# Unread matmuls at the start, gate columns before value products, pooling tiles at the head of the fill, and the first half's last rows two products sooner, in a two-layer decoder trunk

## The chip, the cores and the metric

One Trainium2 chip, one of its cores. The metric is the device time of one execution in microseconds (us). The engines are PE (TensorE: matrix products and transposes), ACT (ScalarE), DVE (VectorE), POOL (GpSimd) and SP (SyncE, which here only issues DMAs).

## The reference, cut to what matters

One inference step of a decoder of two layers, for a prompt of 512 rows and a sample group of 8 x 4 rows that share all weights (544 columns in all; the model's width is 1024, its inner width 2816). All is float32.

```python
h = rmsnorm(x, g_mix)
z = h @ w_in                       # cut by columns among mixers and gates
u_pool, q_raw, kv_raw, nsa_gate, c_b, c_c, c_x, gate_pool, gate_nsa, gate_conv = split_columns(z)
y_pool = pool_mixer(u_pool, ...)   # trailing means over 2/4/8/16 rows, minus the row, a map per group, a scale
y_nsa  = nsa_mixer(q_raw, kv_raw, nsa_gate, ...)  # compressed blocks, selected blocks, window; a gate per head
y_conv = c_b * conv3(c_c * c_x)
merged = sum(sigmoid(gate_b) * (y_b @ w_br_b) for the three branches)
x = x + merged @ w_out
x = x + (silu(conv3(hf @ W_a)) * (hf @ W_b)) @ W_down     # hf = rmsnorm(x, g_ffn)
# after the layers: a final rmsnorm of both groups' rows; caches and states are outputs too
```

## The kernel before, in words

Activations lie with channels on the 128 partitions and the 544 rows of prompt and sample along the free axis, in two halves of 272. A product takes one tile of 128 output channels: for each half and each of the 8 tiles of the 1024 input channels there are three matmuls (L323, L324, L326), since each operand is split into a high and a low part: high x high, high x low, low x high. So a full product is 48 matmuls of 128 x 128 weights and 272 columns.

The program is a list of tasks, which `tasks` makes for each layer. A task is a product, its weights, and a function that takes the result out of PSUM (`evac`). Weights come by a DMA on SP into one of 3 raw buffers, three tasks ahead (`look`); ACT casts the high part (L298), and DVE, or POOL while the attention heads run, subtracts to get the low part (L299). The gate columns of the sparse attention (`zng`, 24 of them) have weights of their own: `stacked_weights` sets a tile to zero on POOL (L316), copies the high part on ACT (L317) and subtracts the low part on DVE (L318), so that each k takes two matmuls. Products accumulate in one of 3 PSUM buffers `g`. There are two buffers each for transposes (`PT`) and for attention scores (`PS`), and 8 work tiles `W`.

The order on PE is written out by hand and is the order in which the program emits. On the other engines a planner sets the order from its own costs; only in `setup` ACT and SP go in written order too. `later(n, ...)` puts work n ticks ahead, and a tick is one half product.

Each layer has three stages. Stage "z": the normalised input's products: zkc, zvc, zks (their start also makes the norm), zkw, four zq, then zvs and zvw (the values of the selected and the window keys), zng (the gate columns), a conv tile c, two cmp products (block compression, from `cmp_split`: L532 casts on ACT and L534 subtractions on DVE, 8 of each, on pages that DMAs L455 bring), a conv tile x, and two cmp products. What stands behind zng: `nsa_gates` evacuates on ACT and DVE (L688, L689, L690), ends with a tanh (L692) and a DVE step (L693); `nsa_rows` transposes on PE (L700) two ticks later.

Stage "fill": conv b of tile j = 0, then c, x, b of j = 1, then pairs of a gate and a branch product (first the eight of the conv branch, then the pooling branch). These are pumped between the steps of the attention: first the sample's (L729 to L803; `L767`, `L769`, `L771` scale, the transposes L776 read), then 8 heads, with a fixed amount of product time per step. The two pooling tiles zpool stand in it behind six gates. `pool_mix` evacuates them (L643 to L645 on DVE), adds shifted copies of the columns on POOL (L654 and L655), and makes mean minus token on DVE (L662 to L667); `pool_map` follows 9 and 10 ticks later.

Stage "rest": the branch products of the attention, `w_out`, and the FFN in chunks of ups and downs. In the last chunk of the last layer the eight down products are made by halves: first half 0 of all eight, then half 1. `final_tile` adds the residual (L1238) and sums squares (L1246). `final_sum` gives 1/rms by Newton steps on DVE (L377 to L383); `final_rows` spreads them over the rows with a PE product (L393), multiplies on POOL (L1262) or DVE (L1264) and stores (L1266). `fl` holds how many half 1 products stand between half 0's last product and its `final_sum` and `final_rows`.

Of the kernel before, what the change touches and what calls it, by code (L numbers as in the profile page):

```python
# [6 lines left out]
F32 = mybir.dt.float32  # L7
F32R = mybir.dt.float32r
# [8 lines left out]
NP = 512  # L17
# [199 lines left out]
class Task:  # L217
    def __init__(self, name, evac, w, x, m, pre, mode, stage, halves, keep):
        self.name, self.evac, self.w, self.x, self.m = name, evac, w, x, m
        self.pre, self.mode, self.stage, self.halves, self.keep = pre, mode, stage, halves, keep  # L220
# [1 line left out]


class Trunk:
    def __init__(self, tc, ins, outs, ctx, slots=49, work=8, fill=1.66, look=3, lag=3, np_=4, nps=2, pm=9, ng=3, raw=3, by_pool=((0, 1, 2, 3, 4, 5, 6, 7), (1, 3, 5)), fl=(2, 7, 6, 1), ys=(4.0, 3.0, 10.0, 3.0, 3.0, 3.5)):
        self.tc, self.nc, self.i, self.o = tc, tc.nc, ins, outs
        pool = lambda name, **k: ctx.enter_context(tc.tile_pool(name=name, **k))
        self.cp = pool("cp", bufs=1)
        self.wp = pool("wp", bufs=4)
        self.bp = pool("bp", bufs=3)  # L230
        self.tp = pool("tp", bufs=slots)
        self.kp = pool("kp", bufs=work)
        self.dp = pool("dp", bufs=1, space=bass.MemoryType.DRAM)
        self.sp = pool("sp", bufs=2)
        self.ps = pool("ps", bufs=1, space=bass.MemoryType.PSUM)
        self.n = 0
        self.ng, self.raw = ng, raw
        self.by_pool, self.fl, self.ys_ = by_pool, fl, ys
        self.np_, self.nps, self.pm = np_, nps, pm
        self.fill, self.look, self.lag = fill, look, lag  # L240


    def nm(self, p):
# [155 lines left out]
    def setup(self):  # L399
        nc, i = self.nc, self.i  # L400
        self.cst = self.cp.tile([128, CS_W], F32, name="cst")
        self.norms = self.cp.tile([128, NM_W], F32, name="norms")
        self.ones = self.cp.tile([128, 2], F32, name="ones")
        self.vc = self.cp.tile([128, 256], F32R, name="vc").rearrange("p (g n) -> p g n", g=2)
        self.cT = self.cp.tile([128, 512], F32R, name="cT")
        self.ptt = self.cp.tile([1, 16], I32, name="ptt")
        self.cst1 = self.cst2 = None
        nc.vector.memset(self.ones, 1.0)
        nc.scalar.activation(self.ones[:, 1:2], self.ones[:, 0:1], AF.Tanh)
        self.x = [self.T() for _ in range(KT)]  # L410
        self.ident = self.c("ident")
        nc.gpsimd.memset(self.vc[64:128].bitcast(F32), 0.0)
        nc.gpsimd.memset(self.cT[64:128].bitcast(F32), 0.0)
        s, v, g = nc.scalar, nc.vector, nc.gpsimd
        by = ((s, None), (s, v), (g, None), (s, v), (s, v), (g, g), (s, v), (s, v))
        ap = self.tl[0].w[0]
        r = self.raw_weights(8)
        for t, a in ((self.norms, i["norms"]), (self.x[0], i["xT"][:, 0]), (r[:, 0:4], ap[:, 0:4]),
                     (self.x[1], i["xT"][:, 1]), (r[:, 4:8], ap[:, 4:8])):
            nc.sync.dma_start(t, a)  # L420
        for k in range(2, 7):
            nc.sync.dma_start(self.x[k], i["xT"][:, k])
        self.norm_tile(0, 0, "g_in")
        w = self.weight_parts(r, 0, 4)
        self.norm_tile(1, 0, "g_in")
        self.got[0] = w + self.weight_parts(r, 4, 8)
        self.nxt = 1
        for k in range(2, 7):
            self.norm_tile(k, 0, "g_in")
        for k in range(3):  # L430
            self.square_sum(self.x[k], k, *by[k])
        self.ahead(2)
        nc.sync.dma_start(self.x[7], i["xT"][:, 7])
        nc.sync.dma_start(self.cst, i["cst"])
        nc.sync.dma_start(self.ptt, i["pt"])
        for u in range(3, 7):
            self.square_sum(self.x[u], u, *by[u])
        self.norm_tile(7, 0, "g_in")
        self.square_sum(self.x[7], 7, *by[7])
# [522 lines left out]
    def tasks(self, l):  # L962
        nc, i = self.nc, self.i
# [3 lines left out]
        def add(name, evac, w, x=h, m=128, pre=None, mode=None, stage="rest", halves=(0, 1), keep=None):  # L967
            T.append(Task(f"{name}.{l}", evac, w, x, m, pre, mode, stage, halves, keep))

        def zt(m):  # L970
            return (i["w_in"][l, m], 8)

        def store(name, j, t):
            nc.sync.dma_start(self.o[name][l, j], t)
# [63 lines left out]
        def raw_v(name, out, j, e0):  # L1038
            def evac(ps):
                z = self.z_raw(ps)  # L1040
                store(out, j, z)
                nc.gpsimd.tensor_copy(self.Ev[:, :, e0:e0 + 4], self.seq4(z))
                self.later(2, lambda: setattr(self, name, self.v_stack(z)))
            return evac

        add("zvs", raw_v("vsel", "kvT", 3, 16), zt(8), stage="z")
        add("zvw", raw_v("vwin", "wT", 1, 20), zt(9), stage="z")

        def gates(ps):
            z = self.nsa_gates(ps)  # L1050
            self.later(2, lambda: self.nsa_rows(z))
            self.later(3, self.nsa_sample)

        add("zng", gates, (i["w_ng"][l], 8), m=64, stage="z")
        self.hid = [None] * 2

        def cmp(st, a):
            def evac(p):
                if a == 1:
                    self.hid[st] = self.gelu(p)  # L1060
            return evac

        def conv(j, nme):
            def evac(ps):
                self.zz[nme] = self.z_raw(ps)
                if nme == "b":
                    self.yc[j] = self.conv_mix(j, self.zz["c"], self.zz["x"], self.zz["b"])
                    if j == 1:
                        nc.sync.dma_start(self.o["co"][l], self.coO)
            return evac  # L1070

        for j in range(2):
            for u, nme in enumerate("cxb"):
                add("zconv", conv(j, nme), zt(10 + 3 * j + u), stage="z" if j == 0 and u < 2 else "fill")
                if j == 0 and u < 2:
                    for a in range(2):
                        add("cmp", cmp(u, a), (i["cw1"][l, u][:, 8 * a:8 * a + 8], 8),
                            x=lambda a=a: self.cmpx[8 * a:8 * a + 8],
                            pre=(lambda st=u: self.cmp_split(st)) if a == 0 else None, mode=f"cmp{a}", stage="z")


        def gate(key, m):
            def evac(ps):
                t = self.T() if self.mg[m] is None or key == "n" and m > 1 else self.W()
                self.halves(ps, lambda p, cs: nc.vector.tensor_mul(t[:, cs], p, self.r[:, cs]))
                nc.scalar.activation(t, t, AF.Tanh, scale=0.5)
                self.gt[key, m] = t
            return evac
# [12 lines left out]
                    nc.gpsimd.tensor_add(self.mg[m], self.mg[m], t)  # L1101
            return evac

        def pool(j):
            def evac(ps):
                pd = self.pool_mix(j, ps)
                for hf in range(2):
                    self.later(self.pm + hf, lambda hf=hf: self.pool_map(j, pd, hf))
            return evac

        kinds = {"c": (18, 0, lambda: self.yc), "p": (26, 2, lambda: self.yp), "n": (34,)}
        seq = [(key, m) for key in "cp" for m in range(8)]
        for n, (key, m) in enumerate(seq + [("n", 0)]):
            if n == 6:
                for j in range(2):
                    add("zpool", pool(j), zt(16 + j), stage="fill")
            add("gate", gate(key, m), zt(kinds[key][0] + m), stage="fill")
            if n > 0:
                key, m = seq[n - 1]
                k0, x = kinds[key][1:]  # L1120
                add("branch", branch(key, m), (i["br_a"][l, m, :, k0:k0 + 2], 2), x=x, stage="fill")
# [303 lines left out]
```

## Time and profile before

| | |
|---|---|
| median of 3 runs (lowest, highest) | 1763.63 us (1761.86, 1764.05) |
| the profiled execution's own time | 1759.85 us |
| its span in the profile | 1758.0 us |
| PE, PE weight load, DVE, ACT, POOL busy | 97%, 96%, 65%, 42%, 28% |
| chain that ended last, by engine | PE 87%, DVE 7%, SP's queue 2%, DMA 2% |
| DMA | 175.52 MB, 100 GB/s on average |

How to read it: the span runs from the profile's start to its last event, and the execution's time is a little more. Busy shares are of the span; loading of weights into PE overlaps its matmuls. Engines wait for each other through semaphores; the profile infers what ended a wait.

### The profile page before, as it was taken

The page shows a single profiled execution, that of the slowest core. Times are in us where ns is not written, and L with a number is a line of the kernel's source. Part 1 is how long each engine was busy: PE and PEld are TensorE (multiplying, and loading weights), DVE is VectorE, ACT ScalarE, POOL GpSimd, SP SyncE. Part 2 cuts the span into 40 slices and gives each one's busy share as a digit, 9 for nine tenths or more (in the row PEclk, how much of TensorE's full clock was granted, in tenths as well). Part 3 has the DMA queues.
Part 4 walks back from the last instruction along what each step waited for, and adds up shares of the span by engine and source line. Part 5 has one row for each costly group of instructions (what it writes and reads, how often), then busy time and mean ns, then how long its engine had stood idle before and what let it go on. Part 6 is the DMA issues. An engine that isn't in the chain of part 4 may idle for free.

```text
span 1758.0 us, 35101 instructions
## 1 busy us (share of the span) xinstructions
PE 1710.2 (97%) x13488; PEld 1689.6 (96%) x13488; DVE 1145.0 (65%) x2552; ACT 737.2 (42%) x1499; POOL 487.4 (28%) x719
## 2 busy tenths in 40 slices
PE   8999989999999999999998998999999999999996
PEld 8999989999999999999998998999999999999996
DVE  6675888856566565565857568887564665565566
ACT  5443555643333233233435345666333333232333
POOL 3212655630122121121231226456001321121113
PEclk9999999999999999999999999999999999999998
DMA  6653211224222322322465532112242222323322
GB/s 216 178 183 113 68 47 46 64 78 150 89 85 74 107 77 86 100 77 77 152 176 148 186 116 49 46 49 64 78 153 90 86 83 91 91 79 97 91 75 78
DMA packets 97208, 175.52 MB, mean 100 GB/s; under 512 B 31250, under 2 KB 51858, under 8 KB 97042
## 3 DMA queue, kind: packets, MB, share of 16 engines
q1 hardware_dynamic: 97042, 173.29, 32.5%
q8 instruction: 107, 1.75, 0.4%
q14 instruction: 59, 0.48, 0.1%
HBM read 157.19 MB, written 12.71 MB: 97 GB/s over the span
## 4 chain that ended last, share of the span: by engine, by line
PE 87%; DVE 7%; SPq 2%; DMA 2%; ACT 1%; issue 1%; POOL 0%; DVEq 0%; ACTq 0%; POOLq 0%
PE pg L323 25%; PE pg L324 25%; PE pg L326 25%; PE ps L830 2%; PE po L910 2%; PE pt L872 2%; SPq L483 1%; SPq L455 1%; DVE mx L846 1%; PE ps L323 1%; PE ps L324 1%; PE ps L326 1%; PE ps L1328 1%; PE ps L1329 1%; PE ps L1330 1%
## 5 line engine op out<-in xcount | busy, mean ns | idle before, releaser
L323 PE MATMUL pg<-t,wh 128*128 128x272 f32 x3824 | 1122.1, 294 | 19.8 <-DVE t L1093 8.3
L324 PE MATMUL pg<-t,wh 128*128 128x272 f32 x3824 | 1104.5, 289 | 0.7 <-DVE t L1225 0.7
L326 PE MATMUL pg<-t,wl 128*128 128x272 f32 x3792 | 1097.3, 289 | 0.0
L323 PEld LDWEIGHTS pg<-t,wh 128*128 128x128 f32 x3824 | 722.7, 189 | 24.6 <-DVE t L1093 8.8
L324 PEld LDWEIGHTS pg<-t,wh 128*128 128x128 f32 x3824 | 723.2, 189 | 2.4 <-DVE t L1225 1.0
L326 PEld LDWEIGHTS pg<-t,wl 128*128 128x128 f32 x3792 | 718.1, 189 | 0.2 <-DVE wl L299 0.2
L298 ACT CAST wh<-wr 128x512 fp32r<-128x512 f32 (+2 forms) x528 | 316.8, 602 | 581.8 <-PE pg L324 464.1
L299 DVE TENSOR_TENSOR wl<-wr,wh 128x512 fp32r<-128x512 f32 (+2 forms) x432 | 299.9, 696 | 164.8 <-ACT wh L298 146.3
L1139 DVE TENSOR_TENSOR t<-t,pg 128x272 f32<-128x272 f32 x204 | 89.1, 437 | 99.4 <-PE pg L326 97.6
L1176 POOL TENSOR_TENSOR W<-W,W 128x512 f32<-128x512 f32 x44 | 78.1, 1776 | 229.6 <-ACT wh L298 200.7
L299 POOL TENSOR_TENSOR wl<-wr,wh 128x512 fp32r<-128x512 f32 (+1 forms) x96 | 114.7, 1197 | 70.1 <-ACT wh L298 64.0
L616 POOL COPY t<-W 128x2 f32<-128x2 f32 x44 | 9.9, 225 | 369.6 <-DVE W L1159 333.0
L859 POOL TENSOR_SCALAR P<-P,ls,gate 128x128 f32<-128x128 f32 (+3 forms) x128 | 79.9, 625 | 95.7 <-DVE ls L857 61.4
L852 ACT ACTIVATE P<-ps,mx 128x256 f32<-128x256 f32 (+1 forms) x144 | 71.4, 498 | 45.7 <-DVE mx L846 33.2
L342 DVE TENSOR_TENSOR t<-W,t 128x544 fp32r<-128x544 f32 x48 | 34.9, 727 | 81.2 <-ACT t L341 81.1
L363 POOL TENSOR_TENSOR t<-t,W 128x544 f32<-128x544 f32 x19 | 26.6, 1399 | 207.4 <-ACT W L354 207.4
L874 ACT CAST b<-pt 128x128 fp32r<-128x128 f32 (+3 forms) x128 | 54.0, 422 | 49.7 <-PE pt L872 49.0
L875 DVE TENSOR_TENSOR b<-pt,b 128x128 fp32r<-128x128 f32 (+3 forms) x128 | 62.0, 485 | 16.6 <-ACT b L874 14.9
L830 PE MATMUL ps<-t,Q 128*128 128x288 f32 (+6 forms) x288 | 64.0, 312 | 4.7 <-ACT P L852 3.6
L341 ACT CAST t<-W 128x544 fp32r<-128x544 f32 x48 | 31.1, 647 | 87.0 <-POOL W L1177 82.5
L846 DVE TENSOR_REDUCE mx<-ps 128x1 f32<-128x256 f32 (+1 forms) x144 | 64.5, 448 | 2.3
L1166 ACT ACTIVATE W<-W 128x560 f32<-128x560 f32 x44 | 29.6, 673 | 74.8 <-DVE W L606 74.8
(254 smaller groups left out, 1833.5 us busy)
## 6 DMA issues: line engine op xcount, KB each, us to landing
wr<-up SPq DMA_DIRECT2D x88, 512.0 KB, 3.6
wr<-w_in SPq DMA_DIRECT2D x83, 512.0 KB, 3.8
wr<-down SPq DMA_DIRECT2D x64, 256.0 KB, 2.7
wr<-w_out SPq DMA_DIRECT2D x16, 512.0 KB, 3.6
wr<-down SPq DMA_DIRECT2D x32, 192.0 KB, 2.4
t<-xT SPq DMA_DIRECT2D x16, 272.0 KB, 5.7
b<-pgA SPq DMA_DIRECT2D x64, 64.0 KB, 2.7
wr<-cw SPq DMA_DIRECT2D x8, 512.0 KB, 3.7
```

The costliest lines, as they stand in the source:

```text
L298: nc.scalar.copy(h, r[:, k0:k1])
L299: (eng or nc.vector).tensor_sub(w, r[:, k0:k1], h)
L323: self.nc.tensor.matmul(p[:m, :HF], wh, xh[:, cs], start=a, stop=False)
L324: self.nc.tensor.matmul(p[:m, :HF], wh, xl[:, cs], start=False, stop=b and wl is None)
L326: self.nc.tensor.matmul(p[:m, :HF], wl, xh[:, cs], start=False, stop=b)
L830: nc.tensor.matmul(p[:, :n], q[:, 128 * i:128 * i + 128], kd[:, c0:c0 + n], start=u == 0, stop=u == 1)
L846: nc.vector.tensor_reduce(mx[:, u:u + 1], p[:, c0:c0 + m], axis=AX.X, op=OP.max, negate=True)
L852: nc.scalar.activation(t[:, pos:pos + m], p[:, c0:c0 + m], AF.Exp, bias=mx[:, 0:1], accum_out=ls[:, u:u + 1])
L859: nc.gpsimd.tensor_scalar(t[:, 0:n], t[:, 0:n], ls[:, 0:1], self.gate[:, i, 1 + kk, hd:hd + 1], op0=OP.mult, op1=OP.mult)
L875: nc.vector.tensor_sub(blk(pt)[:, lo][:, ::-1], blk(p)[:, 0:i + 1], blk(pt)[:, hi])
L1139: self.halves(ps, lambda p, cs: nc.vector.tensor_add(self.x[m][:, cs], self.x[m][:, cs], p))
L1176: nc.gpsimd.tensor_mul(f[:, 0:NP], t[:, 0:NP], z[:, 0:NP])
```

## The change

It has four parts. (A) `setup` sets a work tile to 1.0 on DVE and issues 11 matmuls of 128 x 128 weights and 512 columns on it, whose result nobody reads. (B) The task zng stands before zvs and zvw and not behind them. (C) The two zpool tasks stand directly behind conv b of j = 0, the first task of the fill, and not behind the sixth gate; `pool` is only moved up, so that it is defined in time. (D) `fl[1]` is 5 and not 7: `final_rows(0)` is emitted two half 1 products sooner.

```diff
-    ... fl=(2, 7, 6, 1), ys=(4.0, 3.0, 10.0, 3.0, 3.0, 3.5)):
+    ... fl=(2, 5, 6, 1), warm=11, ys=(4.0, 3.0, 10.0, 3.0, 3.0, 3.5)):
...
         self.ident = self.c("ident")
+        warm = self.W(NP, F32R)
+        nc.vector.memset(warm.bitcast(F32), 1.0)
+        p = self.PT()
+        for _ in range(self.warm):
+            nc.tensor.matmul(p, warm[:, 0:128], warm, start=True, stop=True)
...
-        add("zvs", raw_v("vsel", "kvT", 3, 16), zt(8), stage="z")
-        add("zvw", raw_v("vwin", "wT", 1, 20), zt(9), stage="z")
...
         add("zng", gates, (i["w_ng"][l], 8), m=64, stage="z")
+        add("zvs", raw_v("vsel", "kvT", 3, 16), zt(8), stage="z")
+        add("zvw", raw_v("vwin", "wT", 1, 20), zt(9), stage="z")
...
         for j in range(2):
+            if j == 1:
+                for n in range(2):
+                    add("zpool", pool(n), zt(16 + n), stage="fill")
             for u, nme in enumerate("cxb"):
                 add("zconv", conv(j, nme), zt(10 + 3 * j + u), stage="z" if j == 0 and u < 2 else "fill")
...
         for n, (key, m) in enumerate(seq + [("n", 0)]):
-            if n == 6:
-                for j in range(2):
-                    add("zpool", pool(j), zt(16 + j), stage="fill")
             add("gate", gate(key, m), zt(kinds[key][0] + m), stage="fill")
```

## Rows read from the trace of the kernel before

**Rows 1.** The page's line of busy time, share of the span, and instructions.

```profile
PE 1710.2 (97%) x13488; PEld 1689.6 (96%) x13488; DVE 1145.0 (65%) x2552; ACT 737.2 (42%) x1499; POOL 487.4 (28%) x719
```

**Rows 2.** PE's waits: who released it; us in total, times, longest.

```profile
PE pg L323 <- DVE t L1093: 8.3, 2, 4.2
...
PE pt L700 <- DVE W L693: 5.8, 2, 3.3
PE po L393 <- DVE ny L383: 4.1, 1, 4.1
PE pg L323 <- DVE wh L318: 3.8, 2, 2.0
```

**Rows 3.** Stretches: length, busy PE PEld DVE ACT POOL, PEclk, DMA share, GB/s.

```profile
5.98:15.78 9.80, 9.10 (x37) 8.55 (x38) 9.11 (x10) 9.11 (x15) 5.13 (x4) 1.00 0.91 355
...
89.58:94.88 5.30, 5.30 (x26) 5.12 (x24) 5.30 (x11) 5.30 (x9) 0.00 (x0) 0.68 0.30 99
955.60:959.41 3.81, 3.81 (x27) 3.61 (x25) 3.81 (x9) 3.81 (x7) 0.00 (x0) 1.00 0.30 85
232.05:237.64 5.59, 5.59 (x24) 5.56 (x25) 4.25 (x16) 2.63 (x7) 2.29 (x3) 0.50 0.01 4
...
203.00:232.00 29.00, 24.43 (x190) 23.59 (x188) 26.48 (x75) 15.33 (x41) 22.53 (x30) 0.98 0.22 50
...
118.00:142.00 24.00, 24.00 (x201) 22.90 (x200) 14.88 (x38) 11.05 (x28) 8.57 (x19) 1.00 0.45 139
142.00:170.00 28.00, 28.00 (x278) 26.79 (x278) 13.68 (x42) 9.66 (x25) 5.43 (x8) 1.00 0.45 147
1097.24:1101.20 3.96, 3.79 (x17) 3.49 (x18) 3.90 (x14) 1.59 (x4) 1.71 (x2) 0.57 0.01 2
```

**Rows 4.** Instructions at the start: start us, us, engine, line, count, idle before.

```profile
8.82 6.11 DVE L1225 SCALAR_TENSOR_TENSOR t<-t,norms,t 128x544 fp32r<-128x544 f32 x5
```

**Rows 5.** Instructions around the gate columns, and the page's line of their neighbours' DMA.

```profile
71.09 2.95 ACT L532 CAST b<-b 128x326 fp32r<-128x326 f32 x4 [7.36 <-DMA b<-pgA]
73.94 0.35 ACT L317 CAST wh<-wr 128x192 fp32r<-128x192 f32 x1
...
66.80 0.35 SPq L313 DMA_DIRECT2D wr<-w_ng  x1
...
82.99 4.83 DVE L534 TENSOR_TENSOR t<-b,b 128x326 fp32r<-128x326 f32 x7
...
935.50 5.92 ACT L532 CAST b<-b 128x326 fp32r<-128x326 f32 x8 [4.77 <-DMA b<-pgA]
...
wr<-w_in SPq DMA_DIRECT2D x83, 512.0 KB, 3.8
```

**Rows 6.** Lines from 203 to 232 (busy, mean ns), then sample attention's instructions.

```profile
L654 POOL TENSOR_TENSOR W<-W 128x526 f32<-128x526 f32 (+3 forms) x6 | 6.6, 1107 | 0.9 <-DVE pf L645 0.9
...
L662 DVE SCALAR_TENSOR_TENSOR W<-W,W 64x512 f32<-64x512 f32 x4 | 3.7, 936 | 0.1
...
L645 DVE TENSOR_TENSOR pf<-pg,t 128x32 f32<-128x32 f32 x2 | 0.4, 180 | 0.0
...
133.92 2.23 POOL L771 TENSOR_SCALAR W<-W,sfc 128x256 f32<-128x256 f32 x2
137.63 0.60 PE L776 MATMUL pt<-cst,W 128*128 128x128 f32 x4
```

**Rows 7.** Instructions of the last rows, on DVE, PE and POOL.

```profile
1737.42 0.16 DVE L382 TENSOR_TENSOR nt<-nt,nv 128x3 f32<-128x3 f32 x1
...
1737.89 0.15 DVE L383 SCALAR_TENSOR_TENSOR ny<-nt,ny 128x3 f32<-128x3 f32 x1
...
1739.58 0.49 PE L393 MATMUL po<-cst,ny 128*128 128x128 f32 x3
...
1740.75 6.17 POOL L1262 TENSOR_TENSOR W<-t,W 128x272 f32<-128x272 f32 x8 [5.49 <-ACT W L396]
...
1746.26 0.68 DVE L382 TENSOR_TENSOR nt<-nt,nv 128x3 f32<-128x3 f32 x1
```

More of the change, by code (lines that the diff above doesn't have):

```diff
@@ L224, with __init__ @@
 class Trunk:
-    def __init__(self, tc, ins, outs, ctx, slots=49, work=8, fill=1.66, look=3, lag=3, np_=4, nps=2, pm=9, ng=3, raw=3, by_pool=((0, 1, 2, 3, 4, 5, 6, 7), (1, 3, 5)), fl=(2, 7, 6, 1), ys=(4.0, 3.0, 10.0, 3.0, 3.0, 3.5)):
+    def __init__(self, tc, ins, outs, ctx, slots=49, work=8, fill=1.66, look=3, lag=3, np_=4, nps=2, pm=9, ng=3, raw=3, by_pool=((0, 1, 2, 3, 4, 5, 6, 7), (1, 3, 5)), fl=(2, 5, 6, 1), warm=11, ys=(4.0, 3.0, 10.0, 3.0, 3.0, 3.5)):
         self.tc, self.nc, self.i, self.o = tc, tc.nc, ins, outs
@@ L239, in __init__ @@
         self.np_, self.nps, self.pm = np_, nps, pm
-        self.fill, self.look, self.lag = fill, look, lag
+        self.fill, self.look, self.lag, self.warm = fill, look, lag, warm
     def nm(self, p):
@@ L1070, in conv, with pool, evac @@
             return evac
+        def pool(j):
+            def evac(ps):
+                pd = self.pool_mix(j, ps)
+                for hf in range(2):
+                    self.later(self.pm + hf, lambda hf=hf: self.pool_map(j, pd, hf))
+            return evac
         for j in range(2):
+            if j == 1:
+                for n in range(2):
+                    add("zpool", pool(n), zt(16 + n), stage="fill")
             for u, nme in enumerate("cxb"):
@@ L1102, in branch @@
             return evac
[L1104 to L1109, printed above, removed]
         kinds = {"c": (18, 0, lambda: self.yc), "p": (26, 2, lambda: self.yp), "n": (34,)}
```

## The prediction

> **What bounds the kernel now.** I read the busy line first: PE is busy 97% of the span, no other engine over 65%, and a matmul takes 1710.2 / 13488 = 0.127 us [rows 1]. The reader is to see that no product gets shorter here: only PE's idle time, and the time it runs at half clock, can be won. Next the list of what PE waited for [rows 2]: few waits, each with a cause; those of two come in pairs of like size, one per layer. Then a table of stretches [rows 3], for the price of the low clock and for how full the other engines are beside each wait. Last the instructions at each place [rows 4 to 7].
>
> The profiled execution took 1759.85 us (span 1758.0), the median shown is 1763.63, 3.78 more. I form the sum against the profiled one and take it off the median unchanged.
>
> **A. Eleven unread matmuls at the start.** They add a DVE memset and 11 PE instructions ahead of the first product at 5.98, where PE has nothing else. In the first stretch PE issued 37 matmuls in 9.80 us, 9.10 of it busy: 0.246 us each, twice the 0.127 [rows 1, 3], so the start runs at 1.2 GHz, though this row prints 1.00. A matmul of 512 columns in place of 272 is then 0.46 us, eleven 5.1. If the memset is over by 1.2 they end near 6.3, some 0.3 late, or earlier if the clock rises under them. What full clock wins is small, since the x tiles come from DVE: five of them leave it between 8.82 and 14.93 whatever PE does [rows 4]. Only the work after 14.93 gets shorter: until 15.78 these are 3 to 4 matmuls at 0.12 too much each, 0.4 us, and the 0.70 us that the first stretch idles stay. I take +0.3. Ends: +0.7 (the idle time too), and -1.5: PE waits more between those tiles at full clock, and if the clock falls there it costs what the layer 0 stretch below lost.
>
> **B. Gate columns ahead of value products.** The gate product (zng) gets its weights through a POOL memset, the ACT copy L317 and the DVE subtraction L318. In ACT's order L317 stands behind four page casts L532, 2.95 us from 71.09, and runs at 73.94 [rows 5]; PE waits for L318 3.8 us in the two layers [rows 2]. After the product, L693 must give the gate rows to the transposes L700, but seven subtractions L534, 4.83 us from 82.99, are ahead of it on DVE [rows 5]: 5.8 us in two [rows 2]. After layer 0's wait the clock is at half: 26 matmuls took 5.30 us, layer 1's 27 took 3.81 [rows 3], so 1.5. Together 3.8 + 5.8 + 1.5 = 11.1 us.
>
> Two products earlier, zng's weights are wanted before any page cast is due (their DMA, issued at 66.80, goes some 12 us up), and the transposes, two ticks after the product, stand behind all of zvs: L693 has 48 matmuls, 6.1 us, and comes ahead of the L534 block. Both old waits should go. Late next is zvw. L317 ends at 74.3 and PE had then waited nearly 2, so zvw ended near 73; zng now starts two products before, at 61, and with its 32 matmuls and zvs's 48 PE wants zvw at 71. Its DMA takes zng's slot in SP's queue behind the page loads: 66.80 plus 3.8 to landing [rows 5] is 70.6, and a cast and a subtraction (0.74 us each, as one page cast) make it 72: 1 us late per layer. If its cast, or the gates' copies and tanh on ACT, stand behind four page casts, it is 2.95 more, behind all eight 5.92 [rows 5]. I charge 2 per layer, the sure 1 and a third of 2.95: B = 11.1 - 4 = 7. Ends: +11.1, and -4, where both layers pay 5.92 and half of the clock term again (11.1 - 11.8 - 3).
>
> **C. Pooling tiles at the head of the fill.** The two zpool products and their evacuations now stand among the heads, directly before the wait for L1093, 8.3 us in two [rows 2]. From 203 to 232 DVE is busy 26.48 of 29.00 us, POOL 22.53, while PE has 24.43 [rows 3]. Seven pooling lines (L643 to L667; the first and the last by time are shown) are 9.9 us of DVE's [rows 6]. Without them DVE has 16.6 us of work where PE has 24.4: both waits lose their cause. With them goes the half clock behind them: 5.59 us at 0.50 lost 2.8, 3.96 at 0.57 lost 1.7 [rows 3]. Gross 8.3 + 4.5 = 12.8 us.
>
> The new place is behind the first conv b product, in 118 to 170. There DVE has 14.88 of 24.00 and 13.68 of 28.00 us, POOL 8.57 and 5.43 [rows 3]. With 9.9 more, DVE has 38.5 of 52; with six L654 (6.6 [rows 6]), POOL has 20.6: PE's own work covers both. Not covered is what must come on time: sample attention's POOL step L771 ends at 133.92 + 2.23 = 136.15, and the transpose L776 that reads it is at 137.63 [rows 6]. That is 1.5 us of slack; one L654 is 1.1, two in front of it are past it. SP gets two small stores per tile there, and the two tiles' weight loads ahead of the conv and gate weights they change places with: as many in all, so I cost them at nothing; a weight 1 us late would show as a wait for a cast. I charge one miss of 1 us per layer, and 0.5 for the gates that take the pooling tiles' place: 12.8 - 3 = 9.8. Ends: +12.8, and -3, where the wait with its clock only moves and two such misses come on top in one layer and one in the other.
>
> One rule speaks against C. DVE ops beside POOL's adds run long: in the tail L382 took 0.68 us while POOL worked and 0.16 before POOL began [rows 7]. The Trainium skill, "SBUF — State Buffer", section "Who interferes with whom", has it that a DVE instruction with two SBUF inputs and a GpSimd instruction that reads SBUF lock each other out for a whole instruction. The trace agrees by these 0.52 us; by this rule the sum is rival 2's, by the engines' busy shares it is the one below.
>
> **D. First half's last rows two products sooner.** final_rows(0) comes after 5 and not 7 of the second half's eight products. Its eight POOL multiplications L1262 run from 1740.75 for 6.17 us [rows 7], to 1746.92, beside the Newton steps for which PE waits last, 4.1 us [rows 2]. Of these L382 took 0.68 us at 1746.26, but 0.16 when the first half's ran at 1737.42 [rows 7]; I count three steps so stretched, 3 x 0.52 = 1.5. Two products are 2 x 9 x 0.127 = 2.3 us: POOL ends near 1744.6, before these steps, if nothing else runs there. In return PE meets the first half's L393, now at 1739.58, at 1737.3, and the Newton step that it reads ends at 1737.89 + 0.15 [rows 7]: 0.7 late, in PE's own order, so paid in full, unless the steps come earlier too. 1.5 - 0.7 = 0.8, of which I take 0.5, since the moved multiplications meet L1238 and L1246 instead. Ends: +1.5 and -0.8.
>
> **Sum.** 0.3 + 7.0 + 9.8 + 0.5 = 17.6 us: 1742.3 on the profiled execution, 1763.63 - 17.6 = 1746.0 on the median.
>
> **Rivals.**
> - R1, four casts: zvw's cast or the gates' tanh lands behind four page casts in both layers, 2.95 + 1 per layer. B = 11.1 - 8 = 3, time 1750. For it: in layer 1 ACT ran the eight casts in one piece, 5.92 us [rows 5]. Against: in layer 0 the first starts at 71.09, when zng's product has long ended.
> - R2, POOL against DVE: each moved POOL add holds DVE as L382 was held, for its whole length. In 118 to 170 DVE is then taken for 38.5 + 6.6 = 45.1 of 52 us, 87%, near the 91% of the stretch where the wait arose, and a wait of 3.4 us comes per layer. C = 3, time 1753. Against: PE's buffers carry it over single waits, and no head needs DVE at once there.
> - R3, the other side: the planner puts all eight page casts ahead of the gate product's ACT copies. Its two halves hold two of the three g buffers, so zvs's second half stops for 5.9 us, and L693's old wait and zvw's late weights come behind (3.3 + 1): with the half clock of rows 3 (2.8) that is 13 us per layer. Of the gross 11.1 + 10.6 nothing else is touched: 1763.6 - 21.7 + 26 = 1768. It decides from 10.9 us of new wait per layer. For it: ACT's order is the planner's, and the casts start at 935.50 in layer 1. Against: 71.09 in layer 0.
> - R4, C doesn't do what it says: the heads stall with gates in place of pooling, for these bring DVE and ACT work too. C = 0 gives 1756, and 3 us more per layer 1762.
>
> **How the numbers follow.** Forecast 0.55, R1 0.18, R2 0.12, R3 0.07, R4 0.08. The forecast's own range is 1739 to 1750: B from 4 to 11.1, C from 7 to 12.8, not both at an end. R1 and R2 lie at 1750 and 1753 and with one more bad bound at 1758; so 1738 to 1759 leaves out R3, half of R4 and the best sums, under 2 in 10. A measurement of this kernel can't tell less than 0.2%, 3.5 us, from no change. Faster: forecast, R1, R2 and part of R4, less 0.08 for bounds that meet, 0.83. Same: 0.08, R4's rest and the worst of R2. Slower: 0.09, R3 and two bad bounds at once.
>
> **What would show it.** A: the half-clock pace ends before 15.78 and the first product starts near 6. B: no wait for L318 or L693, one of at most 2 us at zvw's first matmul; a wait inside zvs is R3. C: no wait for L1093, full clock from 203 to 240; waits at L776 or behind L654 from 118 to 170 are R2. D: L1262 over before the last Newton steps begin, and these at 0.16. The forecast is wrong if PE idles over 20 us between its first product and its last, or the clock falls more than once before the tail.

## The result and the profile after

The changed kernel takes 1789.71 us (median of 4, 1789.18 to 1792.21), the kernel before beside it 1762.74: ratio 1.0159, 95% interval 1.014 to 1.0179. It is 27 us slower; 17.6 us faster were forecast. The profiled execution took 1789.18 us (span 1786.7).

To see where the time went I took the start of the same PE instruction in both traces, at the seams between stages. (Line numbers shift: L412 to L1045 of the kernel before are five higher in the changed one, so L693 is L698 and L781 is L786; L1093 is L1107; from L1117 on they are four higher, so L1246 is L1250 and L1262 is L1266. The rows of e4 to e12 below have the numbers of the kernel before as far as L1045; e5's L1328 is L1329 of it, the product with what L534 subtracted from the pages.)

| PE instruction at the seam | before | after | lost since the seam above |
|---|---|---|---|
| first sum of the norm, L374 | 23.22 | 22.62 | -0.60 (A) |
| layer 0: end of stage z, L556 | 116.10 | 124.82 | +9.32 (B) |
| first head, L830 | 170.03 | 193.39 | +14.64 (C, new place) |
| last head, L830 | 360.76 | 377.97 | -6.15 (C, old place) |
| layer 0's end, L374 | 889.88 | 906.03 | -1.06 |
| layer 1: end of stage z, L556 | 980.63 | 1007.86 | +11.08 (B) |
| first head, L830 | 1034.65 | 1069.92 | +8.04 (C, new place) |
| last head, L830 | 1225.74 | 1255.63 | -5.38 (C, old place) |
| tail: first half's sum, L374 | 1733.31 | 1762.50 | -0.70 |
| last product, L393 | 1748.45 | 1777.29 | -0.35 (D) |

The sum is +28.8, near the spans' 28.7 (1786.7 - 1758.0). Two things limit how exactly a row can be read. Eight matmuls of `pool_map` per layer, some 1.0 us (estimate: two take about 0.25), moved with C from the old place to the new one, so C won some 9.5 of the 12.8 forecast among the heads, not 11.5, and lost some 20.7 at its new place, not 22.7. And each row sets one execution against one: in the seven other traces with stage z as before (e2, e4, e7, e8, e11, e12, e14 below) PE came through it 0.1 us earlier to 3.2 later in layer 0, and 1.1 to 3.7 later in layer 1, than in the profiled execution of before, which is 2.9 us below its median. So the medians of the experiments decide what a part costs. What the rows do show: B lost where it was to win, C lost more at its new place than it won at the old, and A and D are small.

The page's busy line answers to [rows 1], PE's list of waits to [rows 2]:

```profile
PE 1724.6 (97%) x13499; PEld 1695.4 (95%) x13499; DVE 1149.4 (64%) x2553; ACT 735.0 (41%) x1499; POOL 491.0 (27%) x719
```

```profile
PE pt L705 <- DVE W L698: 10.8, 2, 6.4
...
PE po L789 <- DVE W L786: 4.5, 2, 2.3
PE ps L684 <- DVE W L786: 4.2, 2, 2.2
PE ps L1333 <- DVE t L539: 3.8, 3, 1.8
PE pg L323 <- DVE t L1107: 3.3, 2, 1.6
PE po L393 <- DVE ny L383: 3.2, 2, 2.5
PE pg L323 <- DVE pf L650: 2.7, 1, 2.7
...
PE pg L323 <- DVE W L694: 2.0, 1, 2.0
```

The wait for the gate weights (3.8) is gone; that for the gate rows has grown from 5.8 to 10.8; that behind pooling among the heads has shrunk from 8.3 to 3.3; five new ones of 2 us and more have come. PE's idle time and its busy time both rose by 14.4 us. Of the busy time 1.7 is at the start, with the 11 unread matmuls. The rest is mostly the half clock: by the trace's granted clock it stood at 0.50 for 41.0 us in seven stretches before the tail, against 13.7 us in three before, and PE was busy for 32.6 and 12.2 us of these; half of the difference, some 10 us, is what the low clock added. These are stretches of it, to be set beside [rows 3] (columns as there):

```profile
76.65:83.48 6.83, 4.89 (x24) 4.83 (x25) 2.43 (x6) 2.44 (x5) 0.57 (x2) 0.50 0.68 233
151.74:161.98 10.24, 7.63 (x55) 6.64 (x56) 6.23 (x15) 0.85 (x2) 6.77 (x9) 0.50 0.42 97
957.29:967.53 10.24, 6.70 (x31) 6.39 (x31) 2.70 (x8) 4.05 (x7) 1.35 (x3) 0.50 0.40 134
...
142.00:170.00 28.00, 23.09 (x186) 21.18 (x185) 14.87 (x43) 3.96 (x7) 12.63 (x17) 0.82 0.59 140
```

The first and third come with B's waits, the second with C's. In the last row PE has 23.1 of 28 us where it had all of them before, while DVE is busy only 14.9: what failed there was not DVE's time.

**B's place.** The instructions on ACT, DVE and PE around the gate rows of layer 0, and for ACT of layer 1 too (answer to [rows 5]):

```profile
71.79 5.72 ACT L537 CAST b<-b 128x326 fp32r<-128x326 f32 x8
77.42 0.65 ACT L697 ACTIVATE W<-W 24x544 f32<-24x544 f32 x1
...
954.21 5.54 ACT L537 CAST b<-b 128x326 fp32r<-128x326 f32 x8
959.66 0.65 ACT L697 ACTIVATE W<-W 24x544 f32<-24x544 f32 x1
```

```profile
69.83 0.72 DVE L491 TENSOR_TENSOR t<-t,W 128x544 f32<-128x544 f32 x1 [4.97 <-POOL W L490]
70.48 0.77 DVE L694 TENSOR_TENSOR W<-pg,W 24x272 f32<-24x272 f32 x2
72.00 0.78 DVE L695 TENSOR_TENSOR W<-W,t 24x272 f32<-24x272 f32 x2
...
78.10 0.43 DVE L698 TENSOR_SCALAR W<-W 24x544 f32<-24x544 f32 x1 [0.99 <-ACT W L697]
```

```profile
70.95 0.40 PE L323 MATMUL pg<-t,wh 128*128 128x272 f32 x1 [2.04 <-DVE W L694]
...
78.59 0.62 PE L705 MATMUL pt<-cst,W 24*128 24x24 f32 x4 [4.37 <-DVE W L698]
```

Read from the top of the chain: DVE takes the gate product out of PSUM (L694) only at 70.48, because an add of the last rope (L491) is ahead of it in DVE's order and waits 4.97 us for POOL. Until then two of three g buffers are held, and PE stops inside zvs for 2.04. The rows are ready for the tanh at 72.8; ACT has by then begun eight page casts and runs the tanh behind the last, at 77.42. PE is at the transposes at 74.2 and stands there. Layer 1 goes the same way: an L491 add waits 3.99 us for POOL ahead of the second L694, the tanh runs behind eight casts at 959.66, and PE waits 6.41 us.

**C's place.** DVE, POOL and PE when the second pooling tile comes (answer to [rows 6]):

```profile
146.86 1.05 DVE L672 SCALAR_TENSOR_TENSOR W<-pg,pf 64x32 f32<-64x32 f32 x1
...
151.81 0.19 DVE L650 TENSOR_TENSOR pf<-pg,t 128x32 f32<-128x32 f32 x1 [3.81 <-DMA poS<-pf]
...
152.24 2.29 DVE L299 TENSOR_TENSOR wl<-wr,wh 128x512 fp32r<-128x512 f32 x2
155.47 0.87 DVE L667 SCALAR_TENSOR_TENSOR W<-W,W 64x512 f32<-64x512 f32 x1 [0.94 <-POOL W L659]
156.26 0.41 DVE L786 COPY W<-ps 128x256 f32<-128x256 f32 x1
...
158.49 0.40 DVE L672 SCALAR_TENSOR_TENSOR W<-pg,pf 64x32 f32<-64x32 f32 x2
```

```profile
151.84 0.29 POOL L646 COPY pf<-t 128x120 f32<-128x120 f32 x1 [3.98 <-DMA poS<-pf]
```

```profile
152.15 0.57 PE L323 MATMUL pg<-t,wh 128*128 128x272 f32 x1 [2.72 <-DVE pf L650]
...
156.73 0.80 PE L789 MATMUL po<-W 128*128 128x128 f32 x2 [2.20 <-DVE W L786]
```

The tile pf has one buffer. The first pooling tile's store of it is issued at 143.9 and lands at 151.72; until then DVE and POOL both stand before their writes of the second one, with everything behind them in their order: the evacuation that PE waits for, and then sample attention's copy L786 of what PE transposed at 146.8. It runs at 156.26, behind two weight subtractions and a pooling step that waits for POOL's add L659, and PE waits for it at L789. A third wait comes where `pool_map` asks for a score buffer that sample attention still holds (L684, 4.2 in two).

**The tail** (answer to [rows 7]) and the start:

```profile
1767.41 0.51 PE L393 MATMUL po<-cst,ny 128*128 128x128 f32 x3 [0.69 <-DVE ny L383]
1773.96 0.80 PE L374 MATMUL po<-ones,t 128*128 128x1 f32 x6 [2.67 <-DVE t L1250]
1777.29 0.88 PE L393 MATMUL po<-cst,ny 128*128 128x128 f32 x3 [2.52 <-DVE ny L383]
```

```profile
1775.61 0.16 DVE L382 TENSOR_TENSOR nt<-nt,nv 128x3 f32<-128x3 f32 x1
```

```profile
1.49 4.40 PE L416 MATMUL pt<-W 128*128 128x512 f32 x11 [1.49 <-DVE W L413]
6.25 0.39 PE L323 MATMUL pg<-t,wh 128*128 128x272 f32 x1 [0.36 <-ACT wh L298]
```

PE's last wait is 2.52 in place of 4.1, the one before it 2.67 in place of 2.4, and the new one at the first half's rows is 0.69: 1.6 won, 1.0 given back.

### The profile page after: what moved, and what is told of

It is laid out like the page before. It is cut to its first block, busy times and chain, and to the rows that moved or that the text cites. A ratio compares the mean times of both kernels' runs of the same rounds, so it can differ in the third digit from the quotient of the medians.

```text
span 1786.7 us, 35128 instructions
## 1 busy us (share of the span) xinstructions
PE 1724.6 (97%) x13499; PEld 1695.4 (95%) x13499; DVE 1149.4 (64%) x2553; ACT 735.0 (41%) x1499; POOL 491.0 (27%) x719
## 3 DMA queue, kind: packets, MB, share of 16 engines
q8 instruction: 107, 1.75, 0.4%
## 5 line engine op out<-in xcount | busy, mean ns | idle before, releaser
L323 PE MATMUL pg<-t,wh 128*128 128x272 f32 (+1 forms) x3824 | 1123.1, 294 | 14.3 <-DVE t L1107 3.3
L324 PE MATMUL pg<-t,wh 128*128 128x272 f32 (+1 forms) x3824 | 1102.1, 289 | 2.3 <-DVE t L1229 2.3
L323 PEld LDWEIGHTS pg<-t,wh 128*128 128x128 f32 (+1 forms) x3824 | 722.0, 189 | 21.4 <-issue 4.9
L324 PEld LDWEIGHTS pg<-t,wh 128*128 128x128 f32 (+1 forms) x3824 | 723.2, 189 | 4.6 <-DVE t L1229 3.2
L299 DVE TENSOR_TENSOR wl<-wr,wh 128x512 fp32r<-128x512 f32 (+1 forms) x432 | 303.7, 705 | 172.7 <-ACT wh L298 153.4
```

The lines of the kernel that those rows point to most:

```text
L299: (eng or nc.vector).tensor_sub(w, r[:, k0:k1], h)
L323: self.nc.tensor.matmul(p[:m, :HF], wh, xh[:, cs], start=a, stop=False)
L324: self.nc.tensor.matmul(p[:m, :HF], wh, xl[:, cs], start=False, stop=b and wl is None)
```

## The experiments

Each is the kernel before with one edit, unless said otherwise; the ratio is to the kernel before, run beside it (its median was 1761.60 to 1762.39 us in these).

**Parts alone.** e1 is part B, e2 part C, e8 parts A and D, each with the lines of the diff that belong to it.

> Part B alone (the gate product ahead of the value products; everything else as before). In the changed kernel's trace, PE is 9.3 us later at the end of stage z of layer 0 than at its start, and 11.1 us later over the same stretch of layer 1, against the kernel before. Theory (each part pays for itself): the tanh of the gates stands behind eight page casts on ACT, so B alone costs 9.3 + 11.1 = about +20 us, with the waits for the gate transposes at 4.4 and 6.4 us as in the changed kernel. Rival (the parts hurt each other: the earlier start of PE in A, or C, pushes the casts against the tanh): B alone costs under 5 us, or gains the 7 that were forecast.

Measured: 1779.23 us, ratio 1.0105 (1.0083 to 1.0127), +17.4 us, with waits of 3.1 and 5.3 us at the transposes.

> Part C alone (the two pooling tiles at the head of the fill). From the trace of the changed kernel: 14.7 us lost in layer 0 and 8.1 in layer 1 between the start of the fill and the first head, 6.2 and 5.4 won back among the heads. Theory (each part pays for itself): +22.8 - 11.6 = about +11 us. Rival (it is B's delay that sets sample attention against the pooling tiles): C alone gains, up to the 9.8 us that were forecast, and the waits at the transposes and products of sample attention are under 1 us.

Measured: 1771.89 us, 1.0061 (1.0040 to 1.0083), +10.0.

> Parts A and D alone (unread matmuls at the start, the first half's last rows two products sooner). From the changed kernel's trace: 0.6 us won by the end of the first norm, and 0.4 us between the last products and the end. Theory: -1.0 us, not to be told from before in the total; the start and the tail in the trace show both. Rival (the wait of 0.7 us that PE now has at the first half's product L393 costs what the freed Newton steps win): D is 0 or a loss.

Measured: 1761.93 us, 1.0000 (0.9989 to 1.0011). By the trace, the start won 0.54 us and the tail 0.36, with the same 0.69 us wait at L393.

17.4 + 10.0 - 0.5 = 26.9, and the whole change measured +27.0: within intervals of some 2 to 4 us on each, the parts add, and both rivals that made them hurt each other fall.

**B: what the late tanh costs.** e3 puts the gate product ahead of the four zq; e5 is part B with the readers of the gate rows later; e9 is part B with the page casts on POOL.

```diff
 e3:  add("zng", ...) directly behind add("zkw", ...)
 e5: -self.later(2, lambda: self.nsa_rows(z)); self.later(3, self.nsa_sample)
     +self.later(5, lambda: self.nsa_rows(z)); self.later(6, self.nsa_sample)
 e9: -nc.scalar.copy(hi[:, c], cb[:, :, c::8])
     +nc.gpsimd.tensor_copy(hi[:, c], cb[:, :, c::8])
```

> Part B moved further: the gate product right behind zkw, ahead of the four zq, else as before. Theory: what costs time in B is that the gates' ACT and DVE steps come when the page casts do; some 25 us earlier nothing stands ahead of them, the old waits for the gate weights and for the gate rows (3.8 + 5.8 us and 1.5 of half clock) go and none comes in their place except about 2 us per layer for a conv product's weights or for the first cmp product, which are reached sooner: -5 to -9 us against before. Rival (the pages and their casts are the limit of this stage whatever the order; PE waits for them at the first cmp product): within 2 us of before. Rival (any earlier place breaks the weight order of the zq products): slower by 3 us or more.

Measured: 1767.45 us, 1.0041 (1.0025 to 1.0057), +5.6. The theory missed. The transposes still wait 1.6 and 1.3 us (a rope add is ahead of L693 on DVE), and where no gate work stands before the first cmp product, PE meets it before the page subtractions and waits 1.75 in each layer. The number is the second rival's, but not its reason: no wait for weights stands among the zq products. What came is nearer the first rival, the pages, with two more waits of 1.9 and 1.8 us on evacuations (L475, L481).

> Part B alone, and the transposes of the gate rows put 5 ticks after the gate product in place of 2 (behind the first conv product; sample attention's gate columns 6 in place of 3). PE then doesn't stand at the transposes while the tanh is behind the page casts. Theory (the late tanh is what B costs): the waits of 3.1 and 5.3 us at the transposes and the half clock that follows each (3.4 and 6.8 us at half, 5 us lost) go: 10 to 13 us less than B alone, +4 to +7 against before. Rival (the transposes' wait only stood in for a later one: the first cmp product needs the page subtractions, which DVE does late): PE comes earlier to the first cmp product and waits there for what it no longer waits at the transposes; within 4 us of B alone (+13 to +17).

Measured: 1765.51 us, 1.0015 (1.0003 to 1.0028), +3.1: 14.3 us of B's 17.4 gone by two numbers, a little more than expected. ACT's order is as it was, the tanh behind eight casts (at 78.10); only PE doesn't stand before it. So the theory holds: most of B's cost came because PE read the rows only two ticks after their product. But the wait isn't a gain either: what is left is in part at the first cmp product.

```profile
PE ps L1328 <- DVE t L534: 3.5, 4, 1.4
...
PE pg L323 <- DVE W L689: 2.0, 1, 2.0
```

> Part B alone, with the sixteen page casts per layer on POOL and not on ACT. Theory (the tanh stands behind the page casts in ACT's queue, and PE behind the tanh): ACT is free when the gate rows are ready, the tanh runs near 73 and not 78 us, the waits of 3.1 and 5.3 us at the transposes go or fall under 1 us, and the result is within 4 us of part B with the transposes later (+3 against before). Rival (the gate rows themselves are late, behind the rope add on DVE that waits for POOL): with POOL busier they come later still, the waits at the transposes stay, within 4 us of B alone (+17).

Measured: 1773.96 us, 1.0060 (1.0043 to 1.0076), +12. Neither number. The tanh moved to 74.99, as the theory has it, and the transposes' wait from 8.4 to 4.6; but a cast on POOL takes 1.14 us against 0.74 on ACT, so the subtractions come later, and PE's wait for them at the cmp products went from 4.4 to 7.2. This run can't settle the theory; e5 does.

```profile
L532 POOL CAST b<-b 128x326 fp32r<-128x326 f32 x16 | 17.5, 1140 | 12.4 <-issue 11.0 <-DMA wr<-w_in 1.3
```

**Was there anything to win in B?** e6 is the kernel before with the gate rows read 4 and 5 ticks after in place of 2 and 3; e10 adds the casts on POOL.

> The kernel before, with the transposes of the gate rows 4 ticks after the gate product in place of 2 (behind the first block product cmp), and sample attention's gate columns 5 in place of 3. Theory (the page subtractions are done by then, the first at 83.8 us, so nothing takes the place of the wait for L693): the waits of 3.3 and 2.5 us go, and with them the half clock of layer 0 (1.5): -5 to -7 us against before, which would beat both kernels. Rival (the wait stands in for one on the page casts or subtractions at the first cmp product): within 2 us of before.

Measured: 1762.29 us, 1.0001 (0.9991 to 1.0011). The wait for L693, 5.8 us in [rows 2], is gone, and the kernel isn't faster. What PE waits for in its place:

```profile
PE pg L323 <- ACT wh L298: 8.5, 3, 6.1
...
PE pg L323 <- DVE wh L318: 4.8, 2, 2.4
...
PE pg L326 <- DVE wl L299: 2.5, 2, 1.3
```

6.1 of the first row is the start; 2.4 and 2.5 are the conv x product's weights, whose casts come at 96.49, right behind eight page casts that end there:

```profile
90.50 6.08 ACT L532 CAST b<-b 128x326 fp32r<-128x326 f32 x8 [1.51 <-DVE t L534]
96.49 2.17 ACT L298 CAST wh<-wr 128x512 fp32r<-128x512 f32 x4
```

The rival holds in substance: the wait stood in for another on the page casts, one product on from where the rival had it. (Tried here is a later reader; a value that comes earlier was not tried in this kernel.)

> The kernel before with the transposes of the gate rows 4 ticks after the gate product, and the page casts on POOL. With the transposes alone nothing was won: a wait of 1.1 and 1.2 us for the conv product's weights came, their cast being behind the second eight page casts on ACT. Theory (the page casts on ACT are what stage z waits for, in whichever place): the gate weights' copy isn't behind four casts any more (2.4 us) nor the conv weights' behind eight (2.4 us), half clock windows go: -5 to -9 us against before. Rival (pages and DVE's subtractions set the first cmp product): the wait goes to the subtractions, within 2 us of before. Rival (POOL's casts run over 1.2 us each and hold the rope's POOL step or the subtractions): slower by 3 or more.

Measured: 1771.29 us, 1.0050 (1.0033 to 1.0067), +9: the third case's number, though a cast took 1.06 us there and not over 1.2. In layer 1 the casts stood ahead of the gate weights' memset on POOL, and PE waited 4.9 us for L318.

**C: what the new place costs.** e4 is part C with two pf buffers; e11 is e4 with more fill behind two steps of sample attention.

```diff
 e4:  -bufs=1 if w >= 90 and tag not in ("cm", "pg") else 2
      +bufs=1 if w >= 90 and tag not in ("cm", "pg", "pf") else 2
 e11: -ys=(4.0, 3.0, 10.0, 3.0, 3.0, 3.5)
      +ys=(4.0, 3.0, 10.0, 6.0, 3.0, 3.5)
```

> Part C alone with two buffers for the small tile pf in place of one, so that the second pooling tile doesn't wait for the store of the first (in the changed kernel POOL and DVE both stood 3.8 us for that store in layer 0, and PE 2.7 behind them). Theory: of C's +11 us the 2.7 us wait goes, and with it most of the layer 0 half clock of 10.2 us (5 us) and of the 2.2 us wait behind it: about 6 to 8 us less than part C alone, near +4 us against before. Rival (DVE and POOL are simply too full there, or lock each other out): within 2 us of part C alone.

Measured: 1768.21 us, 1.0039 (1.0026 to 1.0052), +6.4: 3.7 less than part C alone. The wait for the store is gone. Of the 6 to 8 us expected less came, since the copy L781 still was late:

```profile
PE po L784 <- DVE W L781: 4.7, 2, 2.4
PE ps L679 <- DVE W L781: 4.3, 2, 2.3
```

> Part C alone with two pf buffers, and 6 us of fill in place of 3 behind two of sample attention's steps (ahead of the product L784 that waited 2.4 us in each layer, and ahead of L796). Theory (DVE does pooling work when sample attention's copy L781 is due, and PE stands at L784 for it): the waits at L784 go, with the half clock behind them (3.4 us at half each), -5 to -8 us against part C with two pf (+6.4), which leaves -1 to +2 against before. Rival (DVE is late by more than any such slack, or the wait at pooling's L679 grows): within 2 us of part C with two pf.

Measured: 1761.82 us, 1.0000 (0.9990 to 1.0011): 6.6 less than e4. Both waits left the list, with the half clock between 128 and 300. But nothing is won against before, for the fill that PE now takes earlier is missing behind the last head, where PE waits between 362 and 378 us on ACT, DVE and POOL with no products left to do (2.9 and 2.4 us in these rows, both layers).

```profile
PE pt L872 <- POOL P L859: 2.9, 2, 1.4
PE pt L872 <- DVE b L875: 2.4, 4, 0.7
```

**Another place for the pooling tiles.** e7 moves the first tile three gates ahead; e12 has them behind five and seven gates, with `pm=6`.

```diff
-            if n == 6:
-                for j in range(2):
-                    add("zpool", pool(j), zt(16 + j), stage="fill")
+            if n in (5, 7):          # e7: (3, 6), pm=9
+                j = (5, 7).index(n)
+                add("zpool", pool(j), zt(16 + j), stage="fill")
```

> The kernel before, with the first pooling tile three gates earlier and the second where it was, so that their work on DVE and POOL no longer comes in one block. Theory (the 4.2 us wait among the heads comes from some 10 us of DVE work in one block): each half of it is covered by PE's buffers, the wait and its half clock go: -6 to -12 us against before. Rival (DVE is full there with or without the pooling, R4): within 3 us of before. Rival (the first tile now disturbs the sample attention or the first head as in part C): slower by 3 or more.

Measured: 1768.68 us, 1.0042 (1.0025 to 1.0059), +6.3: the last case. The first tile's work met the first heads, at 183.87 PE waits 2.5 us for a softmax.

> The kernel before, with the first pooling tile one gate earlier and the second one gate later (behind five and seven gates) and pool_map 6 and 7 ticks after, so that their work on DVE comes in two halves without being moved to the sample attention or the first head. Theory (the wait of 4.2 us among the heads comes from one block of DVE work; the earlier split lost because its first tile met the first head): -4 to -10 us against before. Rival (DVE is full among the heads anyway, and what pooling adds there is paid wherever it stands): within 3 us of before, with several waits of 1 to 2.5 us in place of the one.

Measured: 1757.21 us, 0.9966 (0.9952 to 0.9981), -4.8. This beats both kernels. The edit changes two things, the places and `pm`, and no run parts them. The 8.3 us wait is gone; waits for softmax steps are 8.8 us where they were 3.6, but none is over 1.9, and the clock stays at full from 94.9 to 955:

```profile
PE ps L830 <- ACT P L852: 8.8, 9, 1.9
```

```profile
170.00:300.00 130.00, 124.31 (x942) 119.58 (x942) 108.16 (x339) 76.73 (x205) 74.70 (x92) 1.00 0.19 56
```

**Together.** e13 is the changed kernel with the three mends of e5, e4 and e11; e14 is e12 with parts A and D.

> The changed kernel, all four parts, with three mends tried one by one before: gate rows transposed 5 ticks after the gate product (6 for sample attention's), two pf buffers, and 6 us of fill behind two steps of sample attention. Theory (the 27 us are two causes, PE standing at the gate transposes for the late tanh, and sample attention behind the pooling work, and the parts add): part B mended +2.7, part C mended -0.2, A and D -0.5 together: near +2 against before (1764), 25 us less than the changed kernel. Rival (the parts also hurt each other when together, for instance the page casts that now meet the pooling tiles): +8 or more against before.

Measured: 1761.90 us, 0.9998 (0.9987 to 1.0009). All 27 us are gone; nothing is left that only the parts together make.

> The version that beat the kernel before (pooling tiles behind five and seven gates, pool_map 6 ticks after) with parts A and D added. Theory (they add): -4.8 from the pooling tiles, 0 to -1 from A and D: -5 to -6 us against before, ratio near 0.997. Rival (A or D costs something that the earlier run of both could not show): 0.998 or above.

Measured: 1756.24 us, 0.9968 (0.9957 to 0.9980), -5.4 us: the fastest here, not to be told from e12.

## Why the prediction was wrong

- **B, "Both old waits should go. Late next is zvw ... I charge 2 per layer"**: this is the step that failed most, +7 forecast, -17.4 measured (e1). The wait for L318 did go, and zvw's weights weren't late: no wait stands at its first product, in e5 neither, where PE doesn't stand at the transposes before it. The wait for the gate rows grew, through the tanh behind eight page casts and the evacuation behind a rope add. R1 had the tanh behind four casts; R3, with a chance of 0.07, had PE stopped inside zvs and 13 us per layer, but by eight casts ahead of ACT's copies of the gate product. These copies ran in time (64.01 and 65.96 in layer 0). What came, the tanh behind all eight, stood in my working as 5.92 us, and of it I charged a third of four casts. It came in both layers. My argument that in layer 0 the casts start at 71.09, "when zng's product has long ended", left out what stood between product and tanh: L694 comes on DVE in order, behind an add that waits for POOL's half of the rope, which waits for SP's shuffles. I gave L693 "48 matmuls, 6.1 us" and never walked the queue ahead of it.
- **B's gross of 11.1**: most of it wasn't there. I read the list of waits as a list of prizes. e6 took the largest away, the 5.8 us, and won nothing: behind it stood the conv weights' casts, behind the same page casts. For the 3.8 us of L318 no run took it away by itself; in e5 both waits are gone, and it is 3.1 us slower than before.
- **C, "both waits lose their cause"**: right in direction. Among the heads some 9.5 us came back of a gross 12.8, and waits of 1.6 us for L1107 stayed. But no run with C at its new place is faster than before; with its waits mended (e11) it is even.
- **C, "I charge one miss of 1 us per layer"**: some 20.7 us measured in two layers; C as a whole was forecast at +9.8 and measured -10.0 (e2). I looked at sums (DVE 38.5 of 52 us) and at one slack, L771 to L776, which indeed wasn't missed: PE's transposes came on time. What failed was a buffer and two links. The buffer is pf: there is one, and a store held it for 7.8 us, one of the small stores of which I wrote "I cost them at nothing". The two links that I hadn't looked at are the copy behind the transposes and `pool_map`'s score buffer. e4 and e11 took 3.7 and 6.6 us away with them.
- **R2, POOL against DVE**: the stretching is there, L672 took 1.05 us beside a POOL add and 0.2 without, as the Trainium skill's "SBUF — State Buffer", section "Who interferes with whom", would have it for a DVE instruction with two SBUF inputs. Two weight subtractions took 2.29 us beside POOL's adds (152.24) and 1.29 at 78.61, where POOL stood still: a part of why the copy L786 was late. e11 undoes C's loss with the adds in the same place, by giving PE other work ahead of the copy, so the adds don't force the loss; how much of the copy's lateness is theirs isn't shown, for no run took them away.
- **The clock**: I counted 1.5 us of half clock as won in B and 4.5 in C, and charged hardly any for new waits. With new waits of 2 to 6 us there are four more stretches of it, and it cost some 10 us more than before, a third of the whole loss.
- **A**, +0.3: 0.60 in this trace, but that isn't clear of chance. In the eleven other traces without the unread matmuls the seam at 23.22 lies from 0.57 us earlier to 0.56 later; in the four with them it is 0.60 (here) and 0.54 (e8) earlier, 0.22 (e14) and 1.24 (e13) later. That A wins anything isn't shown. In e13 came what I had put at the low end, the clock falling between those tiles.
- **D**, +0.5: 0.35, its terms being 1.55 won at the Newton steps (1.5 forecast), 0.69 lost at L393 (0.7) and 0.3 at L1250 (0.3). From the tail's first seam to its last it takes 14.8 us in three of the four traces with D and 15.15 to 15.39 in the twelve without, so the size was right; in e14, where the clock fell 4.3 us before the last product, it takes 15.4 and D won nothing.
- **The range** was put together as if R2 and R3 excluded each other. Both places failed at once, and no case had that.

## What to carry to other kernels

A wait in PE's list is what a stage loses only if nothing stands behind it: put off the reader of the late value for a trial, and see whether the kernel gets faster, before counting the wait as a gain. Before a product is moved, walk every in-order queue between it and the value that is read (here PSUM evacuation behind a rope add, tanh behind casts, a one-buffer tile behind its own store), since busy shares tell nothing of order. Where a late value can't come sooner, reading it later took a change of two numbers here and gave back 14 of the 17 us that moving its product had cost, though not more.

## What the runs showed of the hardware

The half clock doesn't follow a wait of a given length in the same way each time. In the kernel before, layer 1's wait of 2.47 us for the gate rows left the clock at full [rows 3, 955.60]; in e8, with the same wait of 2.50 us, it stood at half for 6.83 us:

```profile
954.91:961.74 6.83, 6.45 (x27) 6.39 (x28) 6.83 (x14) 6.21 (x9) 0.00 (x0) 0.50 0.26 77
```

PE reaches the end of that stage some 3 us later for it. Eight traces have stage z as before, and in all of them this wait is 2.3 to 2.5 us: no half clock came with it in one (before), 3.4 us of it in four (e7, e11, e12, e14) and 6.8 in three (e2, e4, e8). Whether that is what separates the profiled execution of before (1759.85) from its median isn't shown, for it is the only one of that kernel that was traced. The start with the unread matmuls is as uncertain: in the changed kernel the clock rose at 4.97 and stayed until 76.65, in e13 it rose at 5.92 and fell again at 9.33, and the start lost 1.2 us instead of winning 0.6:

```profile
9.33:16.16 6.83, 6.23 (x23) 5.46 (x24) 6.83 (x7) 6.83 (x12) 4.11 (x4) 0.50 0.88 330
```
